# Eleven runs of TensorE products on tiles of ones, put ahead of a two-layer encoder kernel

## The chip, the cores and the metric

The kernel runs on one core of a Trainium2 chip. The metric is the time of one execution on the device in microseconds (us), lower is better. A core has TensorE (PE in the rows; PEld is its weight load), VectorE (DVE), ScalarE (ACT), GpSimd (POOL) and SyncE (SP), which here only issues transfers. Each engine runs its own queue in order and waits for the others by semaphores.

## The reference

Two layers over 256 tokens of width 1024, in float32. Cut to what matters:

```
def hybrid_layer(x, ...):
    h = rms_norm(x, norm1_g)
    proj = jnp.einsum('bsd,de->bse', h, w_in)
    ...
    y_a = mlstm_branch(aq, ak, av, ao, ag, ...)
    y_b = gqa_branch(bq, bk, bv, ...)
    y_c = natten_branch(cq, ck, cv, ...)
    y_d = diff_branch(dq, dk, dv, ...)
    g = jax.nn.sigmoid(gl).reshape(bsz, s, N_BRANCH, D_MODEL)
    merged = (g[:, :, 0] * (y_a @ w_up_a) + g[:, :, 1] * (y_b @ w_up_b)
              + g[:, :, 2] * (y_c @ w_up_c) + g[:, :, 3] * (y_d @ w_up_d))
    x = x + merged @ w_out
    h2 = rms_norm(x, norm2_g)
    return x + (jax.nn.silu(h2 @ w_ffn_gate) * (h2 @ w_ffn_up)) @ w_ffn_down

for l in range(2):
    x = hybrid_layer(x, l, ...)
return rms_norm(x, final_g)
```

## The kernel before

Nearly all of the work is dense products of the activations with weights that are read from memory once. A product in full precision is made of three products of a faster kind (type float32r): every number is split into a high and a low part, and high·high, high·low and low·high are added up in PSUM. The weights come as a stream of units of 2048 columns, each in two halves of 1024. A half lands in one of four tiles `raw0` to `raw3` (issued on SP's queue); ScalarE copies its high part into one of five tiles `whi0` to `whi4`, VectorE subtracts and leaves the low part in `wlo0` to `wlo4`, and then the `raw` tile is free for the next half. So half number h stands in `whi[h % 5]` and `wlo[h % 5]`. In each product the activations are the stationary operand, 128x128, and the weights are the moving one, 512 columns. Results go to one of three PSUM banks, `dense`, which the rows call `pd`; everything else goes to five banks called `pa`.

The program is written out by a scheduler in Python: it keeps estimates of when each engine is through with what it has been given and puts small pieces of work (transposes, the attention branches) between the dense products by these estimates. So an added instruction on TensorE moves the estimate, and may move pieces that follow.

The part around the change is the start. TensorE needs the input x (256 tokens, in two token tiles of 128), transposed and split into `xT`, before its first dense product. `boundary_chunk(t, c, ...)` does it for half c of the columns of token tile t: four transposes on TensorE (float32), the scaled high part by ScalarE (four instructions), the low part by VectorE (four). To fill the time until x lands, `warm(n)` puts n products of the identity by itself (float32, 128x128) on TensorE, with a result in bank `dense[2]` that nothing reads. The order on TensorE at the start is `warm(5)`, transposes of tile 0, `warm(2)`, transposes of tile 1, `warm(3)`, and then the dense products of half 0. A float32 product has two records in the trace, a transpose or a float32r product one.

`ndist` is a table in bf16 that VectorE writes some time later and branch D reads. `whi[4]` and `wlo[4]` get their first weights with the fifth half (number 4).

Of the kernel before, what the change touches and what calls it, by code (L numbers as in the profile page):

```python
# [11 lines left out]
F32 = mybir.dt.float32  # L12
# [8 lines left out]
D = 1024  # L21
# [5 lines left out]
# scheduling: how far the engines may be queued ahead of the tensor engine, how early a piece may advance, what a  # L27
# result takes to reach another engine
FILL, TOL, LAT = 2.5, 0.1, 0.2

# column offsets inside w_in
# [10 lines left out]
# offsets inside the per-layer parameter tile  # L42
# [5 lines left out]
# per-feature columns: norm1 gain, norm2 gain, convolution taps  # L48
# [3 lines left out]
# offsets inside the constant tile  # L52
# [4 lines left out]
def unit_order():  # L57
    """Weight units of one layer in the order in which the tensor engine uses them."""
    o = []
    for n in PLAN:  # L60
        if n == "bkv":
            o += [("bkv", 0, 0), ("bkv", 1, 0)]
        elif n[0] == "u":
            o += [("up", n[1], int(n[2]))]
        else:
            o += [("in", n, 0), ("in", n, 1)]
    for kh in (0, 1):
        for c in (0, 1):
            o += [("wo", kh, c)]
    for j in range(NFB):  # L70
        o += [("gu", j, 0), ("gu", j, 1)]
        if 1 <= j < NFB - 1:
            o += [("dn", j - 1, 0)]
    o += [("dn", NFB - 2, 0), ("dn", NFB - 1, 0)]
    return o
# [5 lines left out]
class Res:  # L81
    """Free list over persistent tiles."""
# [20 lines left out]
class Track:  # L103
    """Estimates of when the regions of tiles are written and read by what was emitted so far; it only orders the program."""
# [15 lines left out]
    def after(self, who, reads, writes):  # L120
        """Earliest start of an instruction of `who` by the regions it touches."""
        t = 0.0
        for aps, wr in ((reads, False), (writes, True)):
            for ap in aps:
                name, lo, hi = self.region(ap)
                for l, h, w, e, end in self.acc.get(name, ()):
                    if l < hi and lo < h and (w or wr or name[0:2] in ("pa", "pd")) and e is not who:
                        t = max(t, end + self.HOP)
        return t
# [10 lines left out]
class Meter:  # L140
    """Passes instructions on to an engine and keeps an estimate of when it is through with them."""
# [29 lines left out]
def trunk(ctx: ExitStack, tc, x_in, wts, par, parc, cst, dist, t2w, fg, out):  # L171
# [57 lines left out]
    with tc.manual_schedule():  # L229
# [24 lines left out]
        def halves(h):  # L254
            """The first piece is split in two steps, so that the tensor engine can begin after one of them."""
            return (slice(0, 512), slice(512, 1024)) if h == 0 else (slice(0, width(h)),)
# [24 lines left out]
        def step(lst, forced):  # L281
            """Each piece advances once what it issued last is through, as far as the engines have room."""
            for t in list(lst):
                if not forced:
                    if lst is tasks and max(V.until, A.until) > T.until + FILL:
                        return
                    if ready.get(t, 0.0) > T.until + TOL:
                        continue
                before = [e.until for e in (V, A, G)]
                try:  # L290
                    next(t)
                    ready[t] = max([e.until + LAT for e, u in zip((V, A, G), before) if e.until != u] or [0.0])
                except StopIteration:
                    lst.remove(t)

        def slot(forced=False):
            """Everything that goes between two runs of dense products; forced: between no products, for what they need."""
            for r in everyres:
                r.flush()
            now = [p for p in pending if p[0] <= 0]  # L300
            pending[:] = [(p[0] - 1, p[1]) for p in pending if p[0] > 0]
            for _, f in now:
                f()
            # at the start the activations come before the weights that follow
            if state["u"] <= 2:
                step(urgent, forced)
            if not forced:
                state["n"] += 1
                behind = state["hi"] - state["live"] < NH - 1
                if state["n"] % 2 == 0 or behind:  # L310
                    emit_lo()
                if state["n"] % 2 == 1 or behind:
                    emit_hi()
            if state["u"] > 2:
                step(urgent, forced)
            step(tasks, forced)

        def after(eng, t, d=LAT):
            """Starts a piece once the engine is through."""
            ready[t] = eng.until + d  # L320
            urgent.append(t)

        def later(f, d=1):
            """Runs f after d more slots."""
            pending.append((d, f))

        def until(cond):
            """Advances everything else until the condition holds."""
            n = 0
# [11 lines left out]
        class Unit:  # L341
            """One weight unit [128, 2048], kept as two halves."""
# [28 lines left out]
        def blk512(units, lhs, nkt, done):  # L371
            """[256 tokens, 512] product over the units; the last unit runs one token tile after the other."""
# [76 lines left out]
        def boundary_chunk(t, c, gcol, st):  # L449
            """Transposes columns [512c, 512c+512) of token tile t into xT and adds to the sums of squares."""  # L450
# [37 lines left out]
        def yt_ok(b):  # L488
            """A branch takes a tile only if one is left for each branch that comes before it."""
            before = [c for c in BRANCHES[:BRANCHES.index(b)] if "hasyt" not in Bs[c]]  # L490
            return YT.ok(1 + len(before))
# [26 lines left out]
        def a_gates(res):  # L518
            """Gate pre-activations -> a and threshold per token (columns), M as rows (split)."""
# [48 lines left out]
            # w1 rows: [a | B]; w2, w0 rows: zero-padded buffers of the running maximum  # L568
# [34 lines left out]
        def a_head(B, h, pc):  # L603
            """Short convolution of q and k, then both directions of one head."""
# [132 lines left out]
        def soft_item(B, i, kind):  # L737
            """Two score rows (two heads, or the two components of a head) against all queries."""
            # the scores of D come divided by the head's slope, a power of two: the distances are then added as they are
# [107 lines left out]
        def soft_tail(B, i, c, e):  # L847
            """Normalised weights of one head [2 x 128 queries, 256 keys] -> transposed output rows."""
# [16 lines left out]
            # columns [high part | low part] of the values against the high part of the weights, then the high part  # L865
            # of the values against the low part of the weights
# [28 lines left out]
        def pair_src(B):  # L895
            """Blocks [q 2 pairs | k 2 pairs] in token layout; a block is free after its second pair."""
# [54 lines left out]
        def b_main(B):  # L951
# [12 lines left out]
            # sums of squares per head: 8 query heads then 2 key heads, per token tile  # L964
# [76 lines left out]
        def warm(n):  # L1041
            """Keeps the tensor engine's clock up until the first operands are there."""
            for _ in range(n):
                T.matmul(dense[2][:, 0:128], ident, ident, start=True, stop=True)

        st = next_stats()
        g1 = pc2[0][:, C_G1:C_G1 + 8]
# [15 lines left out]
        for l in range(L):  # L1063
# [7 lines left out]
            def tok_evac(B, key, tl=None, halves=False, early=False):  # L1071
# [9 lines left out]
                def done(t, p):  # L1081
                    if halves:
                        if B is Bd:
                            # queries of two heads, times 4 ** (head + 1) / 8
# [19 lines left out]
            def bkv_block():  # L1104
                """Keys and values of B and the gates of A."""
# [25 lines left out]
            def split_v(o, p, t):  # L1131
                """Scaled values, per head [high part | low part]."""
# [92 lines left out]
            # output projection  # L1225
# [28 lines left out]
            # feed-forward  # L1254
# [77 lines left out]
            def final_piece(t, o, n, p):  # L1332
                """Residual and final norm of columns [o, o + n); the last piece of a token tile sends it out."""
# [21 lines left out]
            def last_block():  # L1355
                """The last quarter in two narrow pieces, so that little is left to do after the last product."""
# [12 lines left out]
            # the first half waits longer for the last block's activations, the second ends one token tile after the other  # L1369
# [22 lines left out]
def _layout(inp):  # L1392
    """Host-side layout only: reordering, gathering by static indices, broadcasting of rows."""
    f = {k: np.asarray(v) for k, v in inp.items()}
    # rotary pairs of a head are brought next to each other: [row x1 | col x1 | row x2 | col x2]
# [54 lines left out]
    # neighbourhood bias: entry [p, slot, kc] of a query at column p%64 in row p//64 of its tile  # L1450
# [9 lines left out]
def _consts():  # L1460
    """Tables that depend on shapes alone."""
# [39 lines left out]
```

## Time and profile before

| | |
|---|---|
| median of 2 runs | 1112.38 us (1112.28 to 1112.48) |
| span of the profiled execution, first to last instruction | 1109.9 us |
| what the time has over the span | 2.5 us |
| TensorE busy with matmuls | 98% of the span |

The profile's own execution has no time of its own beside its span; the 2.5 us between the span and the median are taken as what lies around it. A busy record of a matmul overlaps with the next one, so the rate of TensorE is read from the distance between starts, not from the length of a record: in a line of a timeline, a group of n records with length T and single records of length s has its starts (T - s) / (n - 1) apart.

### The profile page before, as it was taken

How to read it: one execution, taken by the hardware profiler on the slowest of the kernel's cores; microseconds unless marked ns; L12 is line 12 of the kernel's file. 1: busy time of each engine (PE TensorE's matmuls, PEld its weight loads, DVE VectorE, ACT ScalarE, POOL GpSimd, SP SyncE). 2: the span in 40 equal slices, each digit the busy share in tenths (PEclk: the TensorE clock that was granted, in tenths of full speed). 3: DMA queues.
4: the chain of work that ended last, by engine and by line, in shares of the span. 5: the costliest groups of instructions: out<-in, count | busy, mean ns of one | idle time of the engine just before them, and what ended most of it. 6: DMA issues, size and time to landing. Idle time of an engine off the chain costs nothing.

```text
span 1109.9 us, 14766 instructions
## 1 busy us (share of the span) xinstructions
PE 1086.8 (98%) x5272; PEld 882.2 (79%) x5272; DVE 767.6 (69%) x1361; ACT 616.5 (56%) x1095; POOL 156.8 (14%) x145
## 2 busy tenths in 40 slices
PE   9999989999999999999999999999999999999997
PEld 7887867888888888888788887778888888888885
DVE  6689779889555755564576978798875666555554
ACT  7665547685444644444467656486853555444443
POOL 0001335054210000000000006152423000000000
PEclk9999989999999999999999999899999999999999
DMA  8444434445555555645544443344456445565551
GB/s 287 153 156 158 148 101 143 154 153 165 193 174 169 190 191 173 204 164 180 187 157 146 159 152 133 115 161 158 140 187 199 162 166 192 184 198 170 190 179 67
DMA packets 52329, 184.80 MB, mean 167 GB/s; under 512 B 6049, under 2 KB 6433, under 8 KB 52257
## 3 DMA queue, kind: packets, MB, share of 16 engines
q1 hardware_dynamic: 50112, 178.57, 48.3%
q10 hardware_dynamic: 2144, 5.31, 1.5%
q8 instruction: 41, 0.67, 0.3%
q14 instruction: 32, 0.25, 0.1%
HBM read 182.80 MB, written 1.05 MB: 166 GB/s over the span
## 4 chain that ended last, share of the span: by engine, by line
PE 77%; issue 13%; DVE 4%; POOL 3%; DMA 1%; ACT 1%; ACTq 0%; POOLq 0%; DVEq 0%
PE pd L166 55%; PE pa L166 22%; DVE sm L166 1%; DVE wlo L166 1%; DVE w L166 1%; DMA x<-in_x_dram 1%; POOL bsm L166 1%; POOL w L166 1%; POOL ktok L166 1%; DVE k L166 1%; DMA raw<-in_wts_dram 0%; POOL sm L166 0%; ACT w L166 0%; DVE rq L166 0%; ACT yt L166 0%
## 5 line engine op out<-in xcount | busy, mean ns | idle before, releaser
L166 PE MATMUL pd<-whi,xT 128*128 128x512 f32 (+1 forms) x1984 | 645.0, 396 | 0.0
L166 DVE TENSOR_TENSOR wlo<-raw,whi 128x1024 fp32r<-128x1024 f32 (+2 forms) x341 | 421.3, 1247 | 106.6 <-ACT whi L166 105.6
L166 PEld LDWEIGHTS pd<-whi,xT 128*128 128x128 f32 x1984 | 371.4, 188 | 86.7
L166 ACT ACTIVATE whi<-raw 128x1024 fp32r<-128x1024 f32 (+2 forms) x341 | 353.7, 1047 | 142.9 <-PE pd L166 91.3
L166 PE MATMUL pd<-wlo,xT 128*128 128x512 f32 (+1 forms) x992 | 387.5, 391 | 0.0
L166 PEld LDWEIGHTS pd<-wlo,xT 128*128 128x128 f32 x992 | 186.5, 188 | 39.4 <-DVE wlo L166 0.3
L166 PE MATMUL pa<-whi,yt 128*128 128x512 f32 x408 | 138.7, 402 | 1.4 <-ACT yt L166 1.4
L166 PEld LDWEIGHTS pa<-whi,yt 128*128 128x128 f32 x408 | 76.6, 188 | 19.7 <-ACT yt L166 1.8
L166 PE MATMUL pd<-whi,yt 128*128 128x512 f32 (+1 forms) x272 | 90.7, 402 | 0.0
L166 PE MATMUL pa<-wlo,yt 128*128 128x512 f32 x204 | 80.6, 395 | 0.0
L166 DVE SCALAR_TENSOR_TENSOR w<-w,pd 128x256 f32<-128x256 f32 x44 | 18.5, 421 | 88.3 <-ACT w L166 88.1
L166 POOL TENSOR_TENSOR st<-st,mhalf 128x2 f32<-128x2 f32 (+1 forms) x6 | 3.9, 656 | 521.6 <-DVE st L166 521.6
L166 ACT ACTIVATE k<-pd,st 128x512 f32<-128x512 f32 (+1 forms) x52 | 31.5, 623 | 56.0 <-PE pd L166 56.0
L166 PEld LDWEIGHTS pd<-whi,yt 128*128 128x128 f32 x272 | 52.4, 194 | 11.9 <-issue 0.4
L166 ACT ACTIVATE w<-pd,st 128x256 f32<-128x256 f32 (+1 forms) x48 | 23.7, 493 | 55.1 <-PE pd L166 52.7
L166 PE MATMUL pd<-wlo,yt 128*128 128x512 f32 (+1 forms) x136 | 54.2, 398 | 0.0
L166 ACT ACTIVATE yt<-pa 128x512 fp32r<-128x512 f32 x34 | 20.3, 598 | 56.2 <-PE pa L166 56.2
L166 PEld LDWEIGHTS pa<-wlo,yt 128*128 128x128 f32 x204 | 38.4, 188 | 8.0
L166 POOL TENSOR_TENSOR acc<-acc,k 128x512 f32<-128x512 f32 x16 | 33.0, 2061 | 80.2 <-DVE k L166 80.2
L166 POOL TENSOR_TENSOR w<-w,sm 128x512 f32<-128x512 f32 x32 | 39.4, 1254 | 21.9 <-DVE sm L166 21.9
L166 ACT ACTIVATE w<-pa 64x256 f32<-64x256 f32 (+3 forms) x66 | 26.7, 409 | 26.7 <-PE pa L166 12.7
L166 DVE TENSOR_TENSOR yt<-pa,yt 128x512 fp32r<-128x512 f32 x30 | 20.7, 689 | 29.1 <-ACT yt L166 29.1
(153 smaller groups left out, 1019.0 us busy)
## 6 DMA issues: line engine op xcount, KB each, us to landing
raw<-in_wts_dram SPq DMA_DIRECT2D x332, 512.0 KB, 3.7
t<-in_t2w_dram ACTq DMA_DIRECT2D x8, 384.0 KB, 3.3
raw<-in_wts_dram SPq DMA_DIRECT2D x8, 272.0 KB, 2.9
pt<-in_par_dram SPq DMA_DIRECT2D x1, 584.0 KB, 7.0
pt<-in_par_dram ACTq DMA_DIRECT2D x1, 584.0 KB, 3.6
out_dram<-k SPq DMA_DIRECT2D x2, 288.0 KB, 2.1
x<-in_x_dram ACTq DMA_DIRECT2D x1, 512.0 KB, 9.7
k<-in_fg_dram ACTq DMA_DIRECT2D x1, 512.0 KB, 3.5
```

The lines of the kernel that those rows point to most:

```text
L166: return f(out, *a, **k)
```

## The change

Two calls stand ahead of the first `warm(5)`: `warm(25)`, and a new function that fills three tiles with ones (`whi[4]`, `wlo[4]` and `ndist`, by VectorE) and then issues 14 products of each of eleven forms, 154 in all, into bank `dense[2]`. Eight forms are float32r with 512 columns: plain, with the moving operand 2 elements further, 16 elements further, as two runs of 256, in pairs of elements taken in turn from the two halves of the tile, with both operands out of the same tile, with 64 stationary columns in place of 128, and at the end the plain form again. Three are narrower: float32r with 384 columns, bf16 with 384 columns, float32r with 256 columns. Nothing reads the results. The rest of the diff takes comments and docstrings out and is not shown.

```diff
+        def measure():
+
+            a, b, h = whi[4], wlo[4], ndist
+            V.memset(a.bitcast(F32), 1.0)
+            V.memset(b.bitcast(F32), 1.0)
+            V.memset(h, 1.0)
+            a2 = a.rearrange("p (a n) -> p a n", a=2)
+            forms = [
+                (b[:, 0:128], a[:, 0:512], 512),
+                (b[:, 0:128], a[:, 2:514], 512),
+                (b[:, 0:128], a[:, 16:528], 512),
+                (b[:, 0:128], a2[:, :, 0:256], 512),
+                (b[:, 0:128], a.rearrange("p (a n w) -> p n a w", a=2, w=2)[:, 0:128], 512),
+                (a[:, 512:640], a[:, 0:512], 512),
+                (b[:, 0:64], a[:, 0:512], 512),
+                (b[:, 0:128], a[:, 0:384], 384),
+                (h[:, 0:128], h[:, 0:384], 384),
+                (b[:, 0:128], a[:, 0:256], 256),
+                (b[:, 0:128], a[:, 0:512], 512),
+            ]
+            for l, r, n in forms:
+                for _ in range(14):
+                    T.matmul(dense[2][0:l.shape[1], 0:n], l, r, start=True, stop=True)
+
         st = next_stats()
+        warm(25)
+        measure()
         g1 = pc2[0][:, C_G1:C_G1 + 8]
         first = [boundary_chunk(t, 0, g1, st) for t in (0, 1)]
         warm(5)
```

In the program's order, the start of TensorE's queue before (`pd_61` to `pd_63` are the three dense banks, `pa_64` to `pa_68` the other five, `whi_134` to `whi_138` and `wlo_139` to `wlo_143` the tiles `whi0` to `whi4` and `wlo0` to `wlo4`):

```order
L166 MATMUL pd_63<-ident 128x128 x5
L166 MATMUL pa_64<-ident,x 128x128 x4
L166 MATMUL pd_63<-ident 128x128 x2
L166 MATMUL pa_65<-ident,x 128x128 x4
L166 MATMUL pd_63<-ident 128x128 x3
L166 MATMUL pd_61<-whi_134,xT 128x512 x4
```

The start of the same queue in the changed kernel:

```order
L166 MATMUL pd_63<-ident 128x128 x25
L166 MATMUL pd_63<-whi_138,wlo_143 128x512 x70
L166 MATMUL pd_63<-whi_138 128x512 x14
L166 MATMUL pd_63<-whi_138,wlo_143 64x512 x14
L166 MATMUL pd_63<-whi_138,wlo_143 128x384 x14
L166 LDWEIGHTS ndist
L166 MATMUL pd_63<-ndist 128x384
```

Thirteen more such pairs on `ndist` follow, 14 products of 256 and 14 of 512 columns, and then the rows of before. Behind them one piece of four transposes (token tile 1, second half of the columns) stands six products earlier than it did. On VectorE, the start of the queue in the changed kernel is:

```order
L166 MEMSET mhalf 128x20
L166 MEMSET lnsc 128x1
L166 MEMSET whi_138 128x1024
L166 MEMSET wlo_143 128x1024
L166 MEMSET ndist 128x384
L166 SCALAR_TENSOR_TENSOR xT<-pa_64,pc_115,xT 128x128 x4
```

The three fills are new and stand ahead of the first split of x; further on the split that belongs to the moved transposes goes ahead of that of the fifth weight half:

```order
 L166 TENSOR_TENSOR wlo_141<-raw_132,whi_136 128x1024
 L166 TENSOR_TENSOR wlo_142<-raw_133,whi_137 128x1024
-L166 TENSOR_TENSOR wlo_143<-raw_130,whi_138 128x1024
 L166 SCALAR_TENSOR_TENSOR xT<-pa_67,pc_115,xT 128x128 x4
+L166 TENSOR_TENSOR wlo_143<-raw_130,whi_138 128x1024
 L166 ISA w_4_73,sm_91<-pt 128x64
```

ScalarE has the same kind of exchange once (the scaling of x ahead of a sum of squares). From there to the end the instructions of every engine stand in the same order in both kernels.

## Rows read from the trace of the kernel before

**Rows 1.** The page: the span and the busy time of each engine.
```profile
span 1109.9 us, 14766 instructions
...
PE 1086.8 (98%) x5272; PEld 882.2 (79%) x5272; DVE 767.6 (69%) x1361; ACT 616.5 (56%) x1095; POOL 156.8 (14%) x145
```

**Rows 2.** The chain that ended last, first 30 us: start, length, what.
```profile
1.66 9.72 DMA x<-in_x_dram
...
11.41 0.66 PE pa L166 x4
```

**Rows 3.** Timeline of TensorE, the first 19 us: start, length, instruction, [idle before].
```profile
1.48 2.50 PE L166 MATMUL pd<-ident 128*128 128x128 f32 x10 [1.48 <-POOL ident masks.py:199]
3.90 1.11 PE L166 MATMUL pa<-ident,x 128*128 128x128 f32 x4
4.80 1.06 PE L166 MATMUL pd<-ident 128*128 128x128 f32 x4
6.84 1.11 PE L166 MATMUL pa<-ident,x 128*128 128x128 f32 x4 [0.98 <-DMA x<-in_x_dram]
7.75 1.49 PE L166 MATMUL pd<-ident 128*128 128x128 f32 x6
8.89 1.78 PE L166 MATMUL pd<-whi,xT 128*128 128x512 f32 x4
...
16.11 0.60 PE L166 MATMUL pa<-ident,x 128*128 128x128 f32 x4
...
19.11 0.63 PE L166 MATMUL pd<-whi,xT 128*128 128x512 f32 x2
```

**Rows 4.** Timeline of ScalarE, the first 16 us.
```profile
4.10 1.28 ACT L166 ACT_TABLE_LOAD   x1 [4.10 <-DMA pc<-in_parc_dram]
5.39 1.14 ACT L166 ACTIVATE xT<-pa,pc 128x128 fp32r<-128x128 f32 x4
8.00 1.14 ACT L166 ACTIVATE xT<-pa,pc 128x128 fp32r<-128x128 f32 x4 [0.32 <-PE pa L166]
14.95 1.06 ACT L166 ACTIVATE whi<-raw 128x1024 fp32r<-128x1024 f32 x1 [0.71 <-DMA raw<-in_wts_dram]
```

**Rows 5.** Timeline of VectorE, the first 19 us.
```profile
0.81 0.07 DVE L166 MEMSET mhalf<- 128x20 f32 x1 [0.81 <-PEq L1490]
10.21 1.21 DVE L166 TENSOR_TENSOR wlo<-raw,whi 128x1024 fp32r<-128x1024 f32 x1
17.92 1.12 DVE L166 SCALAR_TENSOR_TENSOR xT<-pa,pc,xT 128x128 fp32r<-128x128 f32 x4
```

**Rows 6.** Timeline of TensorE between 20 and 26 us: dense products, then transposes.
```profile
21.68 0.39 PE L166 MATMUL pd<-wlo,xT 128*128 128x512 f32 x1
21.91 0.63 PE L166 MATMUL pd<-whi,xT 128*128 128x512 f32 x2
22.38 0.39 PE L166 MATMUL pd<-wlo,xT 128*128 128x512 f32 x1
24.95 1.03 PE L166 MATMUL pa<-ident,acc 128*128 128x128 f32 x8
```

**Rows 7.** Timeline of TensorE near the end: products of 256 columns.
```profile
1100.18 0.28 PE L166 MATMUL pd<-wlo,yt 128*128 128x256 f32 x1
1100.30 0.40 PE L166 MATMUL pd<-whi,yt 128*128 128x256 f32 x2
1100.54 0.28 PE L166 MATMUL pd<-wlo,yt 128*128 128x256 f32 x1
```

**Rows 8.** Busy times in two stretches, with the granted clock behind the brackets.
```profile
146.75:157.00 10.25, 7.47 (x18) 5.55 (x19) 7.96 (x18) 3.03 (x6) 2.10 (x2) 0.50 0.30 102
696.30:703.10 6.80, 6.65 (x16) 4.91 (x17) 4.53 (x13) 1.35 (x3) 0.00 (x0) 0.50 0.23 77
```

**Rows 9.** Timeline of TensorE inside the first of these stretches.
```profile
153.70 1.05 PE L166 MATMUL pd<-whi,yt 128*128 128x512 f32 x2
154.55 0.63 PE L166 MATMUL pd<-wlo,yt 128*128 128x512 f32 x1
```

## The prediction

> **What bounds the kernel now.** I first read the page for the busiest engine: TensorE is busy 98% of a span of 1109.9 us [rows 1]. Since busy records overlap, I next read the distance between starts in a dense stretch: three products of 512 columns take 0.70 us from 21.68 to 22.38, 0.233 us each, with no gap between them [rows 6]. So a product that is put on TensorE in such a stretch costs its full distance, and one put ahead of it delays all that follows, unless TensorE had to wait there anyway.
>
> The change sits at the start, so the question is how much idle time there is to fill. The chain of work that ended last begins with the transfer of x, 9.72 us until 11.38 [rows 2]. That looks like ten free microseconds, but the timeline of TensorE shows otherwise [rows 3]: the first pieces of x are there at 3.90 and 6.84, the dense products begin at 8.89, and after the 1.48 us at the very start the idle time before a row is 0.98 us at most. The fillers in between are not needed for the result. So the cover is what lies between 1.48 us, where TensorE starts, and the place from which it runs densely; below I work out how much of it the change can use.
>
> Last, the clock. Four float32 records took 1.06 us at 4.80 and six took 1.49 us at 7.75 [rows 3], so two more records cost 0.43, 0.215 us each. Later four take 0.60 us at 16.11 [rows 3] and eight 1.03 us at 24.95 [rows 6]: 0.43 for four more, 0.1075 each. [...] Two later stretches have a granted clock of 0.50 [rows 8]; there the dense products are 0.425 us apart (0.85 from 153.70 to 154.55 for two) [rows 9].
>
> **The change part by part.** *The 25 fillers* are 50 float32 records, since a product has two. TensorE starts them at 1.48 as before (they wait for the identity alone). At the low clock all take 50 x 0.215 = 10.75 us, at the high one 50 x 0.1075 = 5.4 us. They run without a gap, as the fillers and transposes from 6.84 did, so I expect the clock to rise inside them, and take the middle: 8.1 us.
>
> *The fills of ones.* VectorE fills two tiles of 128x1024 and one of 128x384. The fill of 20 columns took 0.07 us and a subtraction over 1024 columns 1.21 us [rows 5], which bound one of them; even at the upper end the three end at 0.9 + 1.2 + 1.2 + 0.5 = 3.8 us, before the earliest end of the fillers (1.48 + 5.4 = 6.9). VectorE's first work of before needs x from ScalarE, after 5.39 [rows 4], and in the changed kernel it comes much later. Cost: nothing; without that cover it would be 3 us.
>
> *Eight forms of 512 columns in float32r*, 14 each, are 112 products of the kind that the kernel itself runs. 112 x 0.233 = 26.1 us. Each has its own weight load, as in the kernel, where it lies under the product before. The shift of the operand, the 64 columns and the operands out of one tile have no rows of their own; I take them at the row of the plain form. The form in pairs reads two elements here and two elements 512 further on. Its nearest row from below is again 0.233 us, since type and count are the same. The only slower streaming that the trace shows is float32, 0.215 us for 128 columns at the high clock (two records), 0.86 us for 512. That bounds the 14 from above, 8.8 us more. I take the lower, the row with the same type.
>
> [...]
>
> *The narrow forms.* Three products of 256 columns take 0.36 us from 1100.18 to 1100.54 [rows 7], 0.12 each: 14 are 1.7 us. For 384 columns I take the middle of 0.12 and 0.233, 0.177 us: 2.5 us in float32r. The trace has no bf16 product; by the same two rows the 14 take between 1.7 and 3.3 us, and I take 2.5. The ones sum to 26.1 + 1.7 + 2.5 + 2.5 = 32.8 us.
>
> *What comes back.* After the ones, TensorE runs the old start again, but with the clock up and x and the first four weight halves long landed. ScalarE's queue paces that part, so I follow it. Its first piece, the scaling of x, began at 5.39, held up by a table load that started at 4.10 [rows 4], 3.9 us after TensorE's first filler. In the changed kernel it begins after five fillers (10 x 0.1075 = 1.1 us) and four transposes (0.60): 1.7 us, 2.2 back. Behind it two waits of ScalarE go, 0.32 us for TensorE and 0.71 us for a weight half [rows 4]: the fifth half is still fetched only after the first has been split, but no other transfer is in its way then. That makes 3.2 us, and VectorE, which before ended the last split of x at 17.92 + 1.12 = 19.04 with TensorE at 19.11 [rows 3, 5], now has that split one place earlier, ahead of a subtraction of 1.2 us, so it does not take it away. I take 3.3. From below the bound is 2.2; from above it is what TensorE alone needs between 1.48 and 19.11: 36 float32 records x 0.1075 and 35 dense products x 0.233 are 12.0 of 17.6 us, 5.6 back.
>
> *The rest* runs in the same order on every engine; the moved transposes and splits cost what they cost before. The two stretches at half clock last 10.25 and 6.80 us [rows 8] though both cover the same work of a layer, so one can come out shorter or longer by 3.4 us when the start shifts, at a loss of 1 - 0.233/0.425 = 0.45 of it, 1.6 us either way.
>
> **Sum.** 8.1 + 32.8 - 3.3 = 37.6 us. On the span: 1109.9 + 37.6 = 1147.5; with the 2.5 us that the median has over the span, 1150.0 us, 3.4% more. A measurement of this kernel can tell about 2% from no change, 22.2 us.
>
> **The rivals.** *The pairs are slow.* [...] Against it: same type and count as the plain form. At the float32 rate 1150.0 + 8.8 = 1158.8 us.
>
> *The clock stays low under the ones.* For it: the fillers and transposes from 1.48 to about 5.9 ran at the low clock to their end [rows 3]. Against it: in the stretch from 6.84, with fillers of the same kind, it rose, and the dense products held it. The price is 32.8 x (0.425/0.233 - 1) = 27.0 us more and 2.65 for the fillers: 1179.7 us.
>
> *The products overlap deeper*, since each starts a new result and none adds to the one before. Then the nearest rate is that of 256 columns, 0.12 us: 112 x 0.113 = 12.7 us less, 1137.3 us, still slower by 2.2%. Against it: the first of every run of dense products in the kernel also starts a new result, and the float32 fillers, which all start new ones, keep the distance of their columns. [...]
>
> *The products never run* (the other side, not slower). Nothing reads them, so a step between program and chip could leave them out. Against it: the fillers of before are not read either, and all 10 products are in the trace with 20 records [rows 3]. Without the ones, the fillers alone add 8.1 - 3.3 = 4.8 us: 1117.2 us. It decides from the point where more than 15.4 of the 32.8 us are gone, some 66 of the 112 wide products.
>
> **How the numbers follow.** My forecast with its own bounds has 0.79, the slow pairs 0.12, the low clock 0.04, the deeper overlap 0.02, the missing products 0.03. The likeliest is 1150.0. Its bounds are the fillers (-2.7, +2.65), the bf16 form (0.8 either way), what comes back (-2.3, +1.1) and the half-clock stretches (1.6 either way); added up, -7.4 and +6.2, so 1142.6 to 1156.2. The slow pairs reach to 1158.8, so the range is 1142 to 1160; it leaves out the other three. All but the missing products are slower by over 2%: 0.97; within 2%: 0.03; nothing here makes it faster.
>
> **What would show it.** In the timeline of the changed kernel, 50 float32 records end near 9.6 us, with distances that fall from 0.215 to 0.1075; then 154 products until about 42.4, at 0.233 for each wide form; ScalarE's first scaling near 44.1, 38.7 us later than before; and from the second unit of weights on everything some 37.6 us late. It is wrong if one form has another distance than its neighbours, if the granted clock is 0.50 under the ones, or if the stretches after 60 us have changed in length.

## The result, and the profile after

The changed kernel takes 1149.08 us (1148.18 to 1149.98, two runs) against 1112.38 us: 1.0336 times the time before, 95% interval 1.0316 to 1.0355. It is slower by 36.7 us; 1150.0 was forecast. The profiled execution took 1148.18 us, with a span of 1146.4 us.

First the timeline of TensorE from the start; these lines answer to [rows 3] and to the dense part of [rows 6]:

```profile
1.48 7.71 PE L166 MATMUL pd<-ident 128*128 128x128 f32 x50 [1.48 <-POOL ident masks.py:199]
8.95 17.91 PE L166 MATMUL pd<-whi,wlo 128*128 128x512 f32 x70
...
42.73 1.28 PE L166 MATMUL pd<-ident 128*128 128x128 f32 x10
43.85 0.60 PE L166 MATMUL pa<-ident,x 128*128 128x128 f32 x4
...
54.19 0.50 PE L166 MATMUL pd<-wlo,xT 128*128 128x512 f32 x1 [0.35 <-DVE wlo L166]
...
56.64 0.63 PE L166 MATMUL pd<-whi,xT 128*128 128x512 f32 x2
```

The fillers take 8.95 - 1.48 = 7.47 us and the ones 42.73 - 8.95 = 33.78. Then the old start follows. The pair of products that began at 19.11 [rows 3] begins at 56.64 here, 37.5 us later. So of 41.25 us put in, 3.7 come back. The wait of 0.35 us at 54.19 is for VectorE's split of a weight half.

The timeline of VectorE and ScalarE at the start, which answers to [rows 4, 5]:

```profile
3.10 0.38 DVE L166 MEMSET ndist<- 128x384 bf16 x1
...
44.49 1.14 ACT L166 ACTIVATE xT<-pa,pc 128x128 fp32r<-128x128 f32 x4 [39.48 <-PE pa L166]
```

The fills end at 3.48, well under the fillers. ScalarE, which set out at 5.39, waits 39.48 us for TensorE and sets out at 44.49, 39.1 later.

To read one form after the other, the ones are cut where a new form starts: stretch, its length, TensorE's busy time (records that touch it), granted clock, share of the transfer engines, GB/s. A stretch holds 14 products, the first 42.

```profile
8.94:18.74 9.80, 9.80 (x45) 1.00 0.22 86
18.74:21.94 3.20, 3.20 (x15) 1.00 0.00 0
21.94:26.68 4.74, 4.74 (x15) 1.00 0.00 0
26.68:29.89 3.21, 3.21 (x15) 1.00 0.00 0
29.89:33.11 3.22, 3.22 (x15) 1.00 0.00 0
33.11:35.57 2.46, 2.46 (x15) 1.00 0.00 0
35.57:37.72 2.15, 2.15 (x15) 1.00 0.00 0
37.72:39.52 1.80, 1.80 (x16) 1.00 0.00 0
39.52:42.73 3.21, 3.21 (x16) 1.00 0.02 5
```

The first row is the plain form and the two shifted ones, 9.80 / 42 = 0.233 us a product. Two runs of 256, one tile for both operands, 64 stationary columns and the plain form again have 3.20 to 3.22 / 14 = 0.229 to 0.230. Only the third row stands out: the form in pairs takes 4.74 / 14 = 0.339 us. 384 columns take 0.176 in float32r; the bf16 form and the 256 columns together take 3.95 us.

The stretches at half clock in the changed kernel (busy times of PE, PEld, DVE, ACT, POOL; clock; transfers), to set beside [rows 8]:

```profile
186.30:193.20 6.90, 6.15 (x15) 4.51 (x16) 4.64 (x13) 1.94 (x3) 0.15 (x1) 0.51 0.30 100
732.40:739.30 6.90, 5.97 (x15) 4.34 (x16) 4.78 (x12) 2.12 (x3) 0.33 (x1) 0.51 0.29 99
```

Both are now of the shorter length; the first of before was 10.25. The span is 36.5 us longer, 1.0 less than the shift after the start: 0.6 of it comes at the first stretch, and 0.4 at the second, which holds 5.97 us of TensorE's work at the low clock where it held 6.65 before [rows 8].

### The profile page after: what moved, and what is told of

It reads as the page before. It is cut to its first block, busy times and chain, and to the rows that moved or that the text cites. A ratio compares the mean times of both kernels' runs of the same rounds, so it can differ in the third digit from the quotient of the medians.

```text
span 1146.4 us, 15178 instructions
## 1 busy us (share of the span) xinstructions
PE 1123.9 (98%) x5476; PEld 911.4 (80%) x5476; DVE 770.3 (67%) x1364; ACT 616.2 (54%) x1095; POOL 157.0 (14%) x145
## 3 DMA queue, kind: packets, MB, share of 16 engines
HBM read 182.80 MB, written 1.05 MB: 160 GB/s over the span
## 4 chain that ended last, share of the span: by engine, by line
PE 79%; issue 13%; DVE 4%; POOL 3%; ACT 1%; POOLq 0%; DVEq 0%
PE pd L166 57%; PE pa L166 22%; DVE sm L166 1%; DVE wlo L166 1%; DVE w L166 1%; POOL bsm L166 1%; POOL w L166 1%; DVE k L166 1%; POOL ktok L166 1%; POOL sm L166 0%; ACT w L166 0%; ACT xT L166 0%; DVE rq L166 0%; ACT whi L166 0%; ACT yt L166 0%
## 5 line engine op out<-in xcount | busy, mean ns | idle before, releaser
L166 ACT ACTIVATE xT<-pa,pc 128x128 fp32r<-128x128 f32 x64 | 18.4, 380 | 55.4 <-PE pa L166 48.3
L166 DVE SCALAR_TENSOR_TENSOR xT<-pa,pc,xT 128x128 fp32r<-128x128 f32 x64 | 17.9, 342 | 44.0 <-ACT xT L166 43.9
```

The source lines that it names most:

```text
L166: return f(out, *a, **k)
```

## The experiments

The theory: a product in TensorE's stream costs the distance to the next one's start and moves all that follows; what comes back is what ScalarE's queue did not need to wait for. Rivals were a cover by the transfer of x, a clock that stays low, and, once the pairs had been seen, ideas of what makes a form slow. Times are compared with runs of the kernel before on the same chip (medians of 1111.1, 1111.5 and 1111.0 us in the timed groups).

**The fillers alone.**

```diff
         warm(25)
-        measure()
```

> The 25 fillers without the ones. My theory: after the fillers ScalarE's first scaling of x paces the start, so they cost what they take (7.5 us in the trace of the changed kernel) less what comes back (3.9 us there): about 3.6 us, 1116.0 us. Rival: they lie under the transfer of x, whose second half lands at 11.4 us, and cost nothing: 1112.4 us. Second rival: nothing comes back, all 7.5 us are paid: 1119.9 us.

Measured: 1115.17 us against 1111.13, 4.0 us more; ratio 1.0036 (1.0024 to 1.0049). The chain that ended last, first 30 us (start, length, what):

```profile
1.48 9.21 PE pd L166 x60
10.69 0.45 PE pa L166 x4
...
11.16 1.14 ACT xT L166 x4
12.30 1.04 ACT whi L166 x2
13.34 1.03 ACT xT L166 x4
```

The transfer of x, which headed this chain before [rows 2], is gone from it; fillers, transposes and then ScalarE without a pause stand in its place. The first rival falls, since half of the fillers' 8.1 us (9.21 less ten records of 0.11) is paid, and so does the second, since the other half is not.

**The ones alone.**

```diff
-        warm(25)
         measure()
```

> The ones without the 25 fillers ahead of them. My theory: products of ones raise the clock as the fillers do; they start at about 3.2 us, when VectorE has filled the tiles, take 33.8 us at the high clock and 1 to 3 us more for a stretch at the low clock, and end 2.5 to 4.7 us earlier than in the changed kernel: 1144.4 to 1146.6 us. Rival: ones do not raise the clock, the fillers did; then the wide products stand 0.425 us apart to their end, 61 us in all, and the time is about 1172 us.

Measured: 1146.33 us, ratio 1.0315 (1.0301 to 1.0329), which is 35.2 us over its own runs of before (the changed kernel: 36.7 over its own). TensorE in two stretches from the start of the ones, columns as above:

```profile
3.12:8.00 4.88, 4.88 (x12) 3.82 (x13) 0.35 (x1) 1.28 (x1) 0.00 (x0) 1.00 0.90 315
8.00:18.38 10.38, 10.38 (x46) 8.47 (x45) 0.00 (x0) 0.00 (x0) 0.00 (x0) 1.00 0.30 118
```

Twelve records in 4.88 us are 0.41 apart, near the 0.425 that goes with a granted clock of 0.50 [rows 8, 9]; 46 in 10.38 are 0.23 apart. (The clock column says 1.00 in both stretches of this trace, so here it is the distances that tell.) So the clock rises under the ones as it does under the fillers, and the rival with a low clock to the end falls. In microseconds as they stand the time lies in the range of the theory; against each kernel's own runs of before the ones alone save 1.5 us, less than the 2.5 to 4.7 expected. The profile shows where the rest is: the line behind the ones, and the two stretches at half clock (busy times as above).

```profile
39.18 1.28 PE L166 MATMUL pd<-ident 128*128 128x128 f32 x10
182.00:192.40 10.40, 8.91 (x23) 6.60 (x24) 7.24 (x15) 2.68 (x5) 0.88 (x1) 0.51 0.26 89
728.20:738.50 10.30, 7.45 (x18) 5.53 (x19) 8.01 (x18) 3.09 (x6) 2.17 (x2) 0.50 0.28 103
```

The ones end at 39.18 where they ended at 42.73, 3.6 us earlier, as the theory has it: they start 1.6 us later than the fillers did and pay for the low clock themselves. But both stretches are of the longer length in this run, with 8.91 and 7.45 us of work at the low clock in place of 6.15 and 5.97. At a loss of 0.45 of the difference that takes back 1.9 us, and the spans differ by 1.6 (1144.8 against 1146.4).

**Half as many products of each form.**

```diff
-                for _ in range(14):
+                for _ in range(7):
```

> Seven products of each form in place of fourteen. My theory: each product costs its distance and nothing else changes: half of 33.8 us less, 1132.2 us. Rival: part of the cost is fixed (a start, a later order of the work): the time falls by less than 15 us, above 1134 us.

Measured: 1132.27 us, ratio 1.0189 (1.0173 to 1.0205). Against the changed kernel's own comparison, 36.7 - 21.1 = 15.6 us fewer where 16.9 were expected; in microseconds as they stand it is 16.8. The line between the two theories, 15 us, is not crossed but not far either, and the runs of before moved by 1.2 us between the two groups. The profile of this run decides (the ones' first line, the line behind them, and the two stretches at half clock):

```profile
8.41 9.08 PE L166 MATMUL pd<-whi,wlo 128*128 128x512 f32 x35
25.38 1.28 PE L166 MATMUL pd<-ident 128*128 128x128 f32 x10
168.10:178.40 10.30, 8.71 (x23) 6.39 (x23) 7.35 (x15) 2.79 (x5) 0.99 (x1) 0.50 0.26 92
714.20:724.60 10.40, 7.39 (x18) 5.47 (x19) 8.10 (x18) 3.26 (x6) 2.33 (x2) 0.51 0.27 101
```

The 77 products take 25.38 - 8.41 = 16.97 us and the 154 took 33.78, so a fixed part is 0.2 us at most. The rest of the difference lies elsewhere: the fillers ended 0.5 us earlier (8.41 against 8.95), and both stretches at half clock are of the longer length, as in the run before, with 4.0 us more work at the low clock than in the changed kernel, a loss of 1.8. 16.8 + 0.5 - 1.8 = 15.5 us, which is what the spans differ by (1146.4 against 1130.9).

**Other strides.** Which part of the form in pairs is slow? `f` is the stationary operand, `a` the tile of ones.

```diff
...
+                f + (a.rearrange("p (a n w) -> p n a w", a=2, w=1)[:, 0:256], 512),
+                f + (a.rearrange("p (a n w) -> p n a w", a=2, w=2)[:, 0:128], 512),
+                f + (a.rearrange("p (a n w) -> p n a w", a=2, w=4)[:, 0:64], 512),
+                f + (a.rearrange("p (a n w) -> p n a w", a=2, w=8)[:, 0:32], 512),
+                f + (a.rearrange("p (n w) -> p n w", w=4)[:, 0:256, 0:2], 512),
+                f + (a.rearrange("p (n w) -> p n w", w=2)[:, 0:512, 0:1], 512),
+                f + (a.rearrange("p (n w) -> p n w", w=2)[:, 0:256, 0:2], 512),
+                f + (a.rearrange("p (n w) -> p n w", w=4)[:, 0:256, 0:1], 256),
...
```

> Other forms of the moving operand in place of the eleven, 14 products each: plain; runs of 1, 2, 4 and 8 elements taken in turn from two halves 2 KB apart; two of every four elements in order; one of every two; pairs that follow each other; one of every four (256 columns); two of every eight (256); plain one element further. [...] Rival, the far jump: only the forms that go to and fro between the halves are slow, two of every four and one of every two stay at 0.23. Second rival, the length of the run: runs of 1 are slowest, one of every two too, and runs of 4 lie between 0.23 and 0.34.

Measured (one run, 1157.82 us): the stretches of runs of 1, 2, 4 and 8, then two of four, one of two, following pairs, one of four (256 columns):

```profile
11.93:14.95 3.02, 3.02 (x15) 2.65 (x14) 0.00 (x0) 0.00 (x0) 0.00 (x0) 1.00 0.02 5
14.95:19.62 4.67, 4.67 (x15) 2.73 (x14) 0.00 (x0) 0.00 (x0) 0.00 (x0) 1.00 0.00 0
19.62:23.12 3.50, 3.50 (x15) 2.66 (x14) 0.00 (x0) 0.00 (x0) 0.00 (x0) 1.00 0.00 0
23.12:26.53 3.41, 3.41 (x15) 2.65 (x14) 0.00 (x0) 0.00 (x0) 0.00 (x0) 1.00 0.00 0
26.53:32.86 6.33, 6.33 (x15) 2.89 (x14) 0.00 (x0) 0.00 (x0) 0.00 (x0) 1.00 0.00 0
32.86:39.19 6.33, 6.33 (x15) 2.90 (x14) 0.00 (x0) 0.00 (x0) 0.00 (x0) 1.00 0.00 0
39.19:42.41 3.22, 3.22 (x15) 2.65 (x14) 0.00 (x0) 0.00 (x0) 0.00 (x0) 1.00 0.00 0
42.41:45.66 3.25, 3.25 (x15) 2.89 (x14) 0.00 (x0) 0.00 (x0) 0.00 (x0) 1.00 0.00 0
```

Divided by 14: 0.216, 0.334, 0.250, 0.244, then 0.452, 0.452, 0.230, and 0.232 for half the columns (two of every eight, also half the columns, took 0.233; the plain form one element further 0.238). Neither the far jump nor the length of the run holds. Single elements taken in turn from two far places were to be slow by both and are the fastest at 0.216 us, faster than the plain form. Leaving elements out in order doubles the time, whether pairs stand together or not: 0.452 us for two of four and for one of two, against 0.230 for pairs that follow each other.

**Distances, then places.** The next two kernels ask what makes the alternating form fast.

```diff
+            def alt(lo, hi, k):
+                return a[:, lo:hi].rearrange("p (a n) -> p n a", a=k)
...
+                f + (alt(0, 1024, 2)[:, 0:256], 512),
+                f + (alt(0, 512, 2), 512),
+                f + (alt(0, 256, 2), 256),
+                f + (alt(0, 512, 4), 512),
+                f + (alt(0, 512, 8), 512),
+                f + (alt(0, 512, 16), 512),
...
```

> Where the run on strides showed 512 columns taken singly from two halves 2 KB apart at 0.216 us, against 0.227 to 0.235 for the plain form: the same with other distances, 14 products each: plain; two places 512 elements apart; two places 256 apart; two places 128 apart (256 columns); 4 places 128 apart; 8 places 64 apart; 16 places 32 apart; 32 places 16 apart; 64 places 8 apart; 128 places 4 apart; two places 256 apart that start 4 elements later. Theory: two neighbours in one place are what costs (0.233 for 512), so every form whose next element is far is at 0.216, down to 16 or 8 elements apart. [...]

Measured (one run, 1165.83 us): two places 512 and 256 apart together (28 products), two places 128 apart (256 columns), then 4, 8 and 16 places:

```profile
12.87:18.91 6.04, 6.04 (x29) 5.29 (x28) 0.00 (x0) 0.00 (x0) 0.00 (x0) 1.00 0.01 3
18.91:20.47 1.56, 1.56 (x15) 1.55 (x14) 0.00 (x0) 0.00 (x0) 0.00 (x0) 1.00 0.00 0
20.47:24.43 3.96, 3.96 (x16) 2.68 (x15) 0.00 (x0) 0.00 (x0) 0.00 (x0) 1.00 0.00 0
24.43:31.28 6.85, 6.85 (x15) 2.90 (x14) 0.00 (x0) 0.00 (x0) 0.00 (x0) 1.00 0.00 0
31.28:37.35 6.07, 6.07 (x15) 2.87 (x14) 0.00 (x0) 0.00 (x0) 0.00 (x0) 1.00 0.00 0
```

Two places are at 0.216 (6.04 / 28) and 0.111 for half the columns; four at 0.283, eight at 0.489, sixteen at 0.434. Of the forms not shown, 32, 64 and 128 places took 0.43 to 0.46, and two places that start 4 elements later 0.217. The theory does not hold: it is not enough that the next element is far, since four places 128 elements apart are at 0.283. Nor are 512 elements between the two places needed, since 256 and 128 do as well. More places came with shorter distances here, so the last kernel separates them:

```diff
+            def two(d, k=2, n=256):
+                v = a[:, 0:512]
+                return bass.AP(tensor=v.tensor, offset=v.offset, ap=[v.ap[0], [1, n], [d, k]])
...
```

> What tells the fast forms from the slow ones, the number of places or the distance. 14 products of 512 columns each: plain; then singly from two places that are 128, 64, 32, 16, 8, 4 and 2 elements apart (256 columns from each, so they overlap where they are near); four places 192 apart; four places 256 apart; eight places 128 apart. Theory, the number of places: two places are at 0.216 us at every distance of more than a few elements, four and eight are slow at every distance (0.28 and 0.49 as before). Rival, the distance: two places get slow from 64 or 32 elements down, and four places 256 apart are at 0.216.

Measured (one run, 1153.92 us): the seven forms with two places in one stretch (98 products), four places 192 and 256 apart (28), eight places 128 apart (14):

```profile
11.86:33.02 21.16, 21.16 (x99) 18.51 (x98) 0.00 (x0) 0.00 (x0) 0.00 (x0) 1.00 0.00 1
33.02:40.90 7.88, 7.88 (x29) 5.37 (x28) 0.00 (x0) 0.00 (x0) 0.00 (x0) 1.00 0.00 0
40.90:47.79 6.89, 6.89 (x15) 2.91 (x14) 0.00 (x0) 0.00 (x0) 0.00 (x0) 1.00 0.01 2
```

21.16 / 98 = 0.216, with no distance between two starts outside 0.215 to 0.217: two places are fast at every distance from 128 down to 2. Four are at 0.281 at both distances, and eight, now 128 apart, at 0.492. So among forms that take single elements in turn the number of places decides. Why two beat one is open.

**Two places for the real weights.** The products of the kernel before, with the weights of each half laid out on the host so that column 2n + a of a block lies at place a:

```diff
-                h = (2 * self.u + c0 // 1024) % NH
-                sl = slice(c0 % 1024, c0 % 1024 + n)
-                return whi[h][:, sl], wlo[h][:, sl]
+                g = 2 * self.u + c0 // 1024
+                h, c = g % NH, c0 % 1024
+                if n == 272 or g == 0:
+                    return whi[h][:, c:c + n], wlo[h][:, c:c + n]
+                q, o = c // 512, c % 512 // 2
+                return tuple(w[h].rearrange("p (a q n) -> p q n a", a=2, q=2)[:, q, o:o + n // 2, :] for w in (whi, wlo))
...
+                    m[:, half] = m[:, half].reshape(128, 2, 256, 2).transpose(0, 3, 1, 2).reshape(128, 1024)
```

> The kernel before with the weights laid out on the host so that each dense product of 512 columns takes its moving operand singly from two places 512 elements apart, the result in the usual order (the first half unit and the narrow products of 272 columns stay plain). My theory: the 0.216 us hold for real data with the other engines at work. 3972 products of 512 columns at 0.0165 us less are 65 us: 1046 us; if VectorE or ScalarE, which now have less time for each weight half, become late in places, up to 1070 us. Rival: the 0.216 us came from idle memory or from the ones; dense products stay at 0.233 us and the time at 1111 us.

Measured: 1050.04 us against 1111.02, ratio 0.9448 (0.9435 to 0.9461), 61.0 us less. The timeline of TensorE in a dense stretch, with VectorE, ScalarE and transfers at work:

```profile
199.87 0.38 PE L166 MATMUL pd<-wlo,xT 128*128 128x512 f32 x1
...
202.03 0.38 PE L166 MATMUL pd<-whi,xT 128*128 128x512 f32 x1
```

Ten products lie between these two starts, (202.03 - 199.87) / 10 = 0.216 us; in these 2.16 us VectorE is busy for 2.10, ScalarE for 1.59, and the transfers move 231 GB/s. The rival falls: the distance is a matter of the access, not of ones or of idle engines. Of the 65 us expected 61 arrived. Who TensorE waits for (total us, times, longest) shows where a part of the rest is:

```profile
PE pa L166 <- DVE w L166: 13.0, 6, 6.1
```

Before, these waits came to 9.9 us, two of them, ahead of the fourth head's scores, 5.0 us at most; with the shorter products they come to 13.0, the longest 6.1.

**Filling the wait.** In each layer TensorE waits for VectorE, 4.96 and 4.95 us, and the granted clock behind the wait is 0.50 [rows 8]. Twenty products of the identity go there, into a bank, `pM`, that the products right behind the scores overwrite; they are issued past the scheduler's estimates, so that the rest keeps its order:

```diff
             pS, pM, e0, e1, dn = PS.get(), PS.get(), W2.get(), W2.get(), SM.get()
+            if h == 3:
+                for _ in range(20):
+                    nc.tensor.matmul(pM[:, 0:128], ident, ident, start=True, stop=True)
```

> The kernel before, with 20 products of the identity (40 records of 0.1115 us, 4.5 us) put where TensorE waits 4.96 us for VectorE, ahead of the scores of the fourth head of branch A in each layer; their result is overwritten by the scores. My theory: idle time there costs twice, since the clock falls in it and the dense products behind stand 0.425 us apart; with the products the clock stays up and the two stretches at half clock, 7.5 and 6.7 us of work, give back 3.4 and 3.0 us: 1106 us. Rival: behind the gap TensorE only runs into the next wait, for weights or for VectorE: 1111 to 1112.4 us. Second rival: the clock falls all the same, since the products keep TensorE less busy than dense ones: 1112.4 us.

Measured: 1105.27 us against 1111.51, ratio 0.9950 (0.9936 to 0.9963), 6.2 us less. TensorE around the first wait:

```profile
144.33 4.63 PE L642 MATMUL pa<-ident 128*128 128x128 f32 x40
149.48 1.13 PE L166 MATMUL pa<-w 128*128 128x256 f32 x4 [0.53 <-DVE w L166]
...
151.78 0.63 PE L166 MATMUL pd<-whi,yt 128*128 128x512 f32 x2
152.24 0.39 PE L166 MATMUL pd<-wlo,yt 128*128 128x512 f32 x1
```

The scores start when they did, but the products behind are 0.23 us apart where they were 0.425 [rows 9]. Both rivals fall.

The same 20 products in the changed kernel:

> The changed kernel with the same 20 products in the same two waits. My theory: its two stretches at half clock go too, about 6 us, to 1143 us; and without them in either kernel the change costs the shift that the start alone has, 37.4 us, so the difference to the kernel before with the products is 37.4 us within 0.3. Rival: the shift of the start is 36.5 to 36.7 us as the times have it, and the stretches took no part: the difference is 36.6 us.

Measured: 1143.57 us, ratio 1.0288 (1.0274 to 1.0302). The difference to the run just told is 38.3 us, 38.7 between the spans, so neither number was hit. The rival's 36.6 is farther off; what I had missed is that the start varies too. In the profiled run the ones begin at

```profile
10.00 2.31 PE L166 MATMUL pd<-whi,wlo 128*128 128x512 f32 x9
```

and not at 8.95: the clock rose later under the same fillers, 1.05 us more. With it, 37.4 is 38.45. The traces bear this out: the pair of products that begins at 17.66 in the run just told begins at 56.24 here, 38.6 later, so the whole difference stands at the start and nothing behind it changes it. That the other three runs rose as late is not shown, since they have no trace.

**The wait made shorter.** The scores one step later:

```diff
+            if h == 3:
+                for _ in range(1):
+                    yield
             while not ("v" in B and "ready" in B["g"] and PS.ok(2) and W2.ok(2) and SM.ok(1)):
```

> The scores one step later alone, without products in the wait. My theory: 1.4 us less in each layer, and the clock still falls in the 3.5 us that are left: 1109.6 us. If the shorter wait is not enough for the clock to fall, 1103 us. Rival: no gain, 1112.4 us.

Measured: 1107.63 us, ratio 0.9964 (0.9952 to 0.9977), 3.9 us less where the theory had 2.8; no gain, the rival, falls. In the profile, whose span is 4.0 us shorter, 1.0 of it stands at the start already: the pair that began at 19.11 [rows 3] begins at 18.16, since the clock rose earlier (the four transposes that took 1.11 us at 6.84 take 0.66 at 6.49). So the two waits give 3.0. The clock still fell (0.992 mean granted, 0.991 before, and 0.998 with the waits filled).

With 14 products in what is left of the wait:

> The kernel before with the fourth head's scores of branch A one step later, behind six more dense products (1.4 us of work that TensorE then does in the wait), and 14 products of the identity in what is left of the wait. My theory: 1.4 us less in each layer beside the 6.4 us of the clock: 1103 us. Rival: the later scores make a later wait of their own and take the 2.8 us back: 1106 us.

Measured: 1102.08 us, ratio 0.9915 (0.9901 to 0.9928), 9.4 us less, as expected (1112.4 - 1103). It is 0.7 short of 6.2 + 3.9, but 1.0 of the 3.9 was the early start in the profile just told. The rival's 1106 falls.

Both with the two places:

> The same with the fourth head's scores one step later and 14 products of the identity in the wait, which took 9.4 us off the kernel before. My theory: the two changes add up, 1037 us. Rival: with dense products that are 7% shorter the waits lie elsewhere or are longer, and the gain is less than half of the 9.4 us: above 1041 us.

Measured: 1042.06 us against 1111.02, ratio 0.9378 (0.9365 to 0.9391). It is 8.0 us below the two places alone, where full addition would give 9.4: mostly additive, and the best kernel of this study, 107 us below the changed one. The time is above the 1041 us that the rival named, but that number was worked out from the 1046 expected of the two places; by its condition, less than half of the gain, the rival falls. Part of what is missing shows in the first layer: with the shorter products, the 14 products in the wait leave TensorE 1.7 us idle, and the clock falls behind that wait (row as above):

```profile
145.80:149.30 3.50, 3.50 (x11) 2.76 (x10) 3.40 (x11) 1.23 (x3) 0.00 (x0) 0.51 0.46 150
```

## Why the prediction was right

- *A product costs its distance.* Right, and carried by the half-sized run. 112 wide products were to take 26.1 us and took 27.4 (the six rows of 512 columns added up); the forms that I took at the plain row stood there. The pairs, taken at the lower of two bounds, lay between them, 0.339 between 0.233 and 0.86: 1.5 us more. Here the prediction was wrong by its own sign, one form with another distance than its neighbours: the rival of slow pairs, given 0.12, was right in kind and far too dear at 8.8 us. The narrow forms took 6.4 for 6.7. The sum of the ones was off by 1.0 us.
- *The fillers.* 8.1 forecast, 7.5 measured, 6.9 in the half-sized run and 8.5 in the one with the filled waits; the middle of the two bounds was fair, since the moment at which the clock rises moves between runs.
- *What comes back.* 3.3 forecast by ScalarE's queue, 3.7 measured. The chain of the run with the fillers alone shows ScalarE pacing the start without a pause, as said, and that run costs 4.0 us. VectorE, which the prediction had out of the way, ends the start all the same: TensorE waits 0.35 us for it at 54.19. The start shift was 37.5 for 37.6 forecast, by errors of -0.6, +1.0 and -0.4 that nearly cancel; that it came within 0.1 is luck, since the fillers alone move by 1.6 us between runs that have the same 25 of them.
- *The stretches at half clock.* The first came out shorter and the second with less work in it, 1.0 us less together, inside the 1.6 that I left open. A changed length after 60 us was another sign that the prediction named against itself, though it had priced it. It seems to vary between runs of one kernel too: the four of the half-sized one have a mean granted clock of 0.989, 0.989, 0.992 and 0.992, and the last two are 1.2 us shorter than the first two. That such stretches are there because TensorE waits, and what they cost, is shown by filling the wait: the products behind are 0.23 us apart in place of 0.425, and the time is 6.2 us less.
- *From span to time.* The prediction added the 2.5 us that the median of before has over its span. In every run with both numbers the difference is 1.7 to 1.9 us (1148.18 against 1146.4), so 0.7 of the 2.5 was a difference between two runs; with 1.8 the forecast would have been 1149.3.
- *The rivals.* The low clock under the ones fell in the trace, with the plain form 0.233 us apart, and by the run without fillers, where 0.41 became 0.23. Deeper overlap fell: the products that add to nothing keep 0.23 us. No product is missing: the changed kernel has 204 records of TensorE more, 50 of fillers and 154 of ones.

## What to carry to other kernels

Work put ahead of this kernel, which TensorE bounds, cost its full time less what the old start wasted (41.25 us put in, 3.7 back). So look for the queue that paces the start and not for the longest transfer. Where TensorE waits some microseconds, count the slower products behind the wait as well: filling the wait with products that are thrown away gave 6.2 us of 1111 here. Before a microsecond is put down to a change, look where the clock rose at the start and how long it stayed low behind a wait: each moved runs with the same work by a microsecond or so here (the 25 fillers took 6.9 to 8.5 us; the half-sized runs at 0.989 mean granted clock took 1.2 us longer than those at 0.992). And measure the access pattern of a moving operand before taking its rate for given: taking single float32r elements in turn from two places, with the weights laid out for it, made each dense product 7% shorter and the kernel 5.5% faster.

## What the runs showed that I had not expected

For 512 columns of float32r at the full clock, 14 products each: 0.216 us from two places singly, 0.23 plain, 0.25 in runs of four, 0.33 to 0.34 in pairs from two places, 0.28 from four places, 0.49 from eight, 0.43 to 0.46 from sixteen and more, 0.45 with every other element left out. An operand's start 1, 2 or 16 elements further made no difference beyond 0.01 us. Where the time goes inside an access stays open; only the count of places and the left-out elements were told apart.
